# A two-layer streaming encoder on one core: part of the query/key group moved to the first pieces, the last piece reordered, one output chunk split in three passes

## The chip, the cores and the metric

The kernel runs on one core of one Trainium2 chip. The metric is the device time of one execution in microseconds. Five engines work beside each other, each on its own queue of instructions in a fixed order: TensorE (PE, with its weight loads as PEld), VectorE (DVE), ScalarE (ACT), GpSimd (POOL) and SyncE (SP), which here issues the large DMAs. A queue's instruction waits for semaphores of the others; what stands behind it waits too.

## The reference

One sequence of 256 tokens, 2048 channels, two layers, float32. All weights are read once, so the kernel streams them. Per layer, cut to what matters:

```python
mod = (c_act @ w_mod[l] + b_mod[l]).reshape(bn, 6, d)      # w_mod: 2048 x 12288
shift_m, scale_m, gate_m = mod[:, 0, None], mod[:, 1, None], mod[:, 2, None]
h = layer_norm(x) * (1.0 + scale_m) + shift_m
proj = h @ w_in[l]
uv, q_c, kv_c, k_r, sb, sc, sh, ag = jnp.split(proj, IN_SPLITS, axis=-1)
y_a = gmlp_mixer(uv, ...)            # gelu, layer norm of v, 128 x 128 mixing over tokens, u * mixed
y_b = mla_mixer(q_c, kv_c, k_r, ...) # latent attention
y_c = short_conv_mixer(sb, sc, sh, sconv_w[l])
y_d = conformer_conv(ag, ...)        # a * sigmoid(g), 31 taps over tokens, layer norm, silu
y = jnp.concatenate([y_a, y_b, y_c, y_d], axis=-1) @ w_out[l]
x = layer_norm(ALPHA * x + (1.0 + gate_m) * y, post_mix_g[l], post_mix_b[l])
...
y = conv_ffn(h, ffn_w_up[l], ffn_w_conv[l], ffn_b_conv[l], ffn_w_down[l])
x = layer_norm(ALPHA * x + (1.0 + gate_f) * y, post_ffn_g[l], post_ffn_b[l])
```

## The kernel before

**Products.** Weights stream in k tiles of 128 rows. A product is either exact (float32 operands, weights straight from DMA in tiles called `wexact`) or 3-pass: the weights arrive in a raw buffer (`wraw`, 4 buffers that the `wmod` transfers share), ScalarE casts them to fp32r (`whi`, L453), VectorE subtracts to get the rest (`wlo`, L454), the activations are split in the same way (`hT`), and three products hi x hi, hi x lo, lo x hi are summed in one PSUM bank. `mm` (L83) records every product.

**Modulation.** `w_mod` is summed over its rows on VectorE: a transfer `wmod`, then steps `qacc` or `macc` (L248) on it; a product with ones and small copies make `mod`, the scale and shift. Layer 0's normalised input needs scale and shift before any product, so it is done in pieces.

**Layer 0 in pieces** (`by_pieces`). `PIECES` cuts the 16 k tiles into (0, 2), (2, 2), (4, 4), (8, 4), (12, 4); a piece waits only for the modulation of its own channels (`between`). In each piece run four column groups: D (w_in's convolution columns, 1024 wide, summed over all pieces in the four PSUM banks `D0_c0` to `D0_c3`), U and V (512 wide each, the gMLP's halves) and E (512 wide, the short convolution's gate). D's products are cut in four parts, with U, V, E between them. The first `PLAIN_KT` = 4 k tiles, pieces 0 and 1, are exact for all groups; the rest of D is 3-pass, and U, V and E are 3-pass only in the last piece. U, V and E do not keep banks between the pieces: `side` computes a piece into two fresh banks, and their running sums lie in SBUF (`sumU`, `sumV`, `sumE`): in piece 0 ScalarE copies the banks there, in middle pieces it copies a bank to `part` (L1289) and VectorE adds (L1290), in the last VectorE adds from the bank (L1286).

**After the pieces** follow `mix_d` (sigmoid `sg` on ScalarE and product `gluD` on VectorE, L869 and L870, then 31 taps), `mix_u` (gelu `ya`, L954) and `mix_v` (gelu `va`, L977; transposed gMLP weights `ps_wT`, `wT`; layer norm; products `ps_mix`). A tap is four products `prodD` on ScalarE (L902) with one add into `convD` on VectorE; the first tap is an ACTIVATE into `convD` itself. There are two `prodD` buffers. The taps lie in the list `background`, from which the later groups pop a few per unit of weights (`STEPS`). Sigmoid and gelu each need their own table in ScalarE (ACT_TABLE_LOAD).

**Group B** (`group` with C_Q, 768 columns: query and key-value latents, exact, banks `B0_c0` to `B0_c2`, 8 units of 2 k tiles), then group C (1024 columns), then the output projection (`out_proj`) in column chunks 0 to 1024, 1024 to 1536 and 1536 to 2048; there `plain` tells how many units of a chunk are exact.

**The rest of w_mod** is spread over the units of these groups: `RATES[0]` tells how many transfers with their `macc` step are issued per unit (`pump`).

The order on each engine's queue is set by a scheduler from the program's order and the dependences.

```python
PIECES = ((0, 2), (2, 2), (4, 4), (8, 4), (12, 4))
CHUNKS = ((0, 1024), (1024, 512), (1536, 512))
rawp = ctx.enter_context(tc.tile_pool(name="rawp", bufs=4))
```

Of the kernel before, what the change touches and what calls it, by code (L numbers as in the profile page):

```python
# [54 lines left out]
def encoder_kernel(ctx: ExitStack, tc: tile.TileContext, A: dict, consts: bass.AP, out: bass.AP):  # L55
# [23 lines left out]
    def acc_tile(name):  # L79
        return accp.tile([P, 512], F32, tag="acc", name=name)  # L80
# [392 lines left out]
        act.copy(hi, src)  # L473
        dve.tensor_tensor(out=lo, in0=src, in1=hi.bitcast(F32), op=ALU.subtract)  # L474

    def group(w, c0, width, name, then, ntm=0, nk=2, hF=None, bg=0, spare=0):

        ncm = (width - 512 * ntm) // P  # L480
        box = {}

        def products(item, u):
            if u == 0:
                box["c"] = [acc_tile(f"{name}_c{i}") for i in range((ncm + 1) // 2)]
                box["t"] = [[acc_tile(f"{name}_t{t}{i}") for i in range(ntm)] for t in range(2)]
                box["h"] = list(hT)
            for part in (range(0, min(4, ncm)), range(4, ncm)):
                for k, (hi, lo) in enumerate(item):
                    kt = u * nk + k  # L490
                    st, sp = kt == 0, kt == KT - 1
                    for i in part:
                        o = box["c"][i // 2][:, (i % 2) * S : (i % 2 + 1) * S]
                        off = slice(i * P, (i + 1) * P)
                        first = st and i % 2 == 0
                        if lo is None:
                            mm(o, hi[:, off], hF(kt), first, sp)
                        else:
                            xh, xl = (h[:, kt % 2, :] for h in box["h"][kt // 2][:2])
                            mm(o, hi[:, off], xh, first, False)  # L500
                            mm(o, hi[:, off], xl, False, False)
                            mm(o, lo[:, off], xh, False, sp)
            for k, (hi, lo) in enumerate(item):
                kt = u * nk + k
                st, sp = kt == 0, kt == KT - 1
                for i in range(ntm):
                    off = slice(ncm * P + i * 512, ncm * P + (i + 1) * 512)
                    for t in range(2):
                        tok = slice(t * P, (t + 1) * P)
                        o = box["t"][t][i]  # L510
                        if lo is None:
                            mm(o, hF(kt)[:, tok], hi[:, off], st, sp)
                        else:
                            xh, xl = (h[:, kt % 2, tok] for h in box["h"][kt // 2][:2])
                            mm(o, xh, hi[:, off], st, False)
                            mm(o, xh, lo[:, off], False, False)
                            mm(o, xl, hi[:, off], False, sp)

        def load(u, spare=spare):
            return weights(w, u * nk, nk, c0, width, hF is not None, spare if u == 0 else 0)  # L520

        def end():
            then(box["c"], box["t"])

        return KT // nk, load, products, end, bg

    def group2(w, c0, name, then, bg=0, spare=0):

# [19 lines left out]
        def load(u):  # L548
            return weights(w, u * nk, nk, c0, 512, False, spare if u == 0 else 0)

        return KT // nk, load, products, lambda: then(box["c"]), bg

    def run(g):
        units, load, products, end, bg = g
        for u in range(units):
            stream(lambda: load(u), lambda item, u=u: products(item, u), bg)
        pending.append(end)

# [684 lines left out]
    def by_pieces(l, w_in, hF, between, mix_d, mix_u, mix_v, mix_b, mix_c, mix_e):  # L1243
# [12 lines left out]
        def terms(kt, part):  # L1256

            hi, lo = part
            if lo is None:
                return [(hi, hf(kt))]  # L1260
            xh, xl = (h[:, kt % 2, :] for h in hT[kt // 2][:2])
            return [(hi, xh), (hi, xl), (lo, xh)]
# [6 lines left out]
                    mm(o, w[:, i * P : (i + 1) * P], x, first and n == 0 and i % 2 == 0, last and n == len(ts) - 1)  # L1269

        def side(g, parts, k0, nkt):
            ps = [acc_tile(f"{g}{l}_{i}") for i in range(2)]
            for kt, part in parts:
                st, sp = kt == k0, kt == k0 + nkt - 1
                if g == "V":
                    ts = terms(kt, part)
                    for t in range(2):
                        for n, (w, x) in enumerate(ts):
                            mm(ps[t], x[:, t * P : (t + 1) * P], w, st and n == 0, sp and n == len(ts) - 1)
                else:  # L1280
                    chan_major(ps, kt, part, range(4), st, sp)
            for i in range(2):
                if k0 == 0:
                    act.copy(sums[g][i], ps[i])
                elif k0 + nkt == KT:
                    dve.tensor_tensor(out=sums[g][i], in0=ps[i], in1=sums[g][i], op=ALU.add)  # L1286
                else:
                    part = tmp_tile("part")
                    act.copy(part, ps[i])  # L1289
                    dve.tensor_tensor(out=sums[g][i], in0=part, in1=sums[g][i], op=ALU.add)  # L1290

        first = between(0)[1]
        first()
        for q, (k0, nkt) in enumerate(PIECES):
# [3 lines left out]

            def load(g, kt):

                c0, width = (C_AG, 1024) if g == "D" else (cols[g], 512)
                nk = min(2048 // width, nkt)
# [38 lines left out]
        def mix_ce(cps, tps):  # L1341
# [162 lines left out]
    for l in range(DEPTH):  # L1504
# [4 lines left out]
        else:  # L1509
# [97 lines left out]
```

## Time and profile before

| | |
|---|---|
| time, median of 3 runs | 2297.42 us (2294.97 to 2298.74) |
| the profiled execution's own time | 2298.88 us |
| its span | 2297.1 us |
| mean TensorE clock granted | 0.987 of full |
| TensorE busy | 97% of the span |
| the five pieces of layer 0 | until about 191 us |
| group B, then C, then output, layer 0 | from about 191, 235 and 327 us; output until about 432 us |
| the rest (feed-forward of layer 0, layer 1) | from about 432 us |

A profile row names the engine, the line, the operation and output<-inputs by the program's names. Times are from the span's start. An exact product shows as two matmul instructions, a 3-pass one as three. Idle time before a row stands in brackets with what ended it. The chain of waits is followed back from the last instruction and shows what the end hung on.

### The profile page before, as it was taken

What the parts mean: (1) busy time and instruction counts of PE and PEld (TensorE: products, weight loads), DVE (VectorE), ACT (ScalarE), POOL (GpSimd) and SP (SyncE); (2) the same over time, 40 slices, a digit from 0 to 9 for tenths busy, and PEclk for the clock granted to TensorE, in tenths of its full rate; (3) what the DMA queues carried; (4) which work ended last, traced back from release to release, by engine and by line L of the source; (5) the groups of instructions that cost most, each with busy time, mean ns of one, the idle gap of its engine ahead of it and who ended that gap; (6) DMA issues with size and microseconds to landing.
All of it is one profiled execution on the core that took longest, in us unless ns stands there. A gap on an engine that the chain in (4) does not pass through costs nothing.

```text
span 2297.1 us, 31478 instructions
## 1 busy us (share of the span) xinstructions
PE 2238.4 (97%) x12387; PEld 1934.1 (84%) x12387; DVE 1790.7 (78%) x2211; ACT 1071.6 (47%) x1597; POOL 34.4 (1%) x65
## 2 busy tenths in 40 slices
PE   6899999999999999999999999999999999999998
PEld 4688886798888888888789999889888888888886
DVE  6878987778888888998977899796676565565676
ACT  2235742335454544544455435545454454454553
POOL 2000000000000000000000000000000000000000
PEclk9899999999999999999999999999999999999999
DMA  9999788777889888898857677875665555555554
GB/s 344 362 340 343 271 321 333 263 278 279 317 303 335 292 326 318 303 354 307 311 186 260 202 238 252 291 260 185 249 243 202 193 178 197 192 193 185 188 195 147
DMA packets 228717, 605.21 MB, mean 263 GB/s; under 512 B 14660, under 2 KB 27188, under 8 KB 210900
## 3 DMA queue, kind: packets, MB, share of 16 engines
q1 hardware_dynamic: 227784, 602.30, 73.7%
q8 instruction: 97, 1.59, 0.3%
q0 software_dynamic: 784, 0.90, 0.1%
q14 instruction: 52, 0.43, 0.0%
HBM read 601.05 MB, written 2.10 MB: 263 GB/s over the span
## 4 chain that ended last, share of the span: by engine, by line
PE 89%; DVE 5%; DMA 3%; issue 1%; ACT 1%; SPq 0%; POOL 0%; DVEq 0%; POOLq 0%; ACTq 0%
PE g_c L83 21%; PE v_c L83 21%; PE d L83 20%; PE o L83 8%; PE D_c L83 4%; PE C_c L83 4%; PE B_c L83 3%; DMA wmod<-in_w_mod_dram 2%; PE U_c L83 1%; DVE wlo L454 1%; PE U L83 1%; PE E L83 1%; PE ps_mod L83 1%; PE E_c L83 1%; DVE qacc L248 1%
## 5 line engine op out<-in xcount | busy, mean ns | idle before, releaser
L453 ACT CAST whi<-wraw 128x1024 fp32r<-128x1024 f32 (+1 forms) x632 | 643.6, 1043 | 780.4 <-PE g_c L83 210.0
L454 DVE TENSOR_TENSOR wlo<-wraw,whi 128x1024 fp32r<-128x1024 f32 (+1 forms) x632 | 750.6, 1214 | 292.2 <-ACT whi L453 278.3
L83 PE MATMUL d<-whi,a 128*128 128x512 f32 x1344 | 390.6, 392 | 0.9 <-ACT whi L453 0.9
L248 DVE SCALAR_TENSOR_TENSOR macc<-wmod,cact,macc 128x2048 f32<-128x2048 f32 (+2 forms) x174 | 353.8, 2033 | 32.3 <-DMA wmod<-in_w_mod_dram 31.7
L83 PE MATMUL v_c<-hT,whi 128*128 128x512 f32 (+1 forms) x1456 | 343.1, 383 | 0.0
L83 PE MATMUL g_c<-hT,whi 128*128 128x512 f32 (+1 forms) x1344 | 313.3, 380 | 0.0
L83 PEld LDWEIGHTS v_c<-hT,whi 128*128 128x128 f32 x1456 | 264.6, 189 | 48.5
L83 PEld LDWEIGHTS d<-whi,a 128*128 128x128 f32 x1344 | 253.2, 189 | 54.6 <-ACT whi L453 2.2
L83 PEld LDWEIGHTS g_c<-hT,whi 128*128 128x128 f32 x1344 | 243.4, 189 | 43.2
L83 PE MATMUL d<-wlo,a 128*128 128x512 f32 x672 | 234.4, 392 | 1.6 <-DVE wlo L454 1.6
L83 PE MATMUL v_c<-hT,wlo 128*128 128x256 f32 x1400 | 190.7, 283 | 0.0
L83 PEld LDWEIGHTS v_c<-hT,wlo 128*128 128x128 f32 x1400 | 183.1, 191 | 6.6
L83 PE MATMUL g_c<-hT,wlo 128*128 128x256 f32 x1280 | 175.8, 283 | 0.0
L83 PEld LDWEIGHTS g_c<-hT,wlo 128*128 128x128 f32 x1280 | 168.2, 191 | 5.9
L83 PEld LDWEIGHTS d<-wlo,a 128*128 128x128 f32 x672 | 127.0, 189 | 30.3 <-DVE wlo L454 3.9
L473 ACT CAST a<-g 128x512 fp32r<-128x512 f32 x132 | 80.8, 619 | 91.0 <-PE d L83 89.3
L83 PE MATMUL o<-whi,a 128*128 128x512 f32 x384 | 112.4, 398 | 0.8 <-ACT whi L453 0.8
L474 DVE TENSOR_TENSOR a<-g,a 128x512 fp32r<-128x512 f32 x132 | 87.7, 685 | 9.5 <-ACT a L473 9.5
L83 PEld LDWEIGHTS o<-whi,a 128*128 128x128 f32 x384 | 73.1, 191 | 17.5 <-ACT whi L453 1.2
L83 PE MATMUL D_c<-hT,whi 128*128 128x256 f32 x432 | 82.0, 290 | 2.8 <-ACT hT L473 2.3
L248 DVE SCALAR_TENSOR_TENSOR qacc<-wmod,cact,qacc 128x1024 f32<-128x1024 f32 (+1 forms) x75 | 80.3, 1070 | 2.6 <-DMA wmod<-in_w_mod_dram 0.5
L1364 DVE SCALAR_TENSOR_TENSOR u<-g,pf,u 128x254 f32<-128x254 f32 (+1 forms) x176 | 73.5, 476 | 3.0 <-ACT u L86 3.0
(371 smaller groups left out, 2603.7 us busy)
## 6 DMA issues: line engine op xcount, KB each, us to landing
wraw<-in_ffn_w_up_dram SPq DMA_DIRECT2D x168, 1024.0 KB, 5.0
wmod<-in_w_mod_dram SPq DMA_DIRECT2D x134, 1024.0 KB, 6.2
wraw<-in_ffn_w_down_dram SPq DMA_DIRECT2D x88, 1024.0 KB, 5.2
wraw<-in_w_in_dram SPq DMA_DIRECT2D x33, 1024.0 KB, 6.9
wmod<-in_w_mod_dram SPq DMA_DIRECT2D x64, 512.0 KB, 9.2
wraw<-in_w_out_dram SPq DMA_DIRECT2D x26, 1024.0 KB, 6.7
wmod<-in_w_mod_dram SPq DMA_DIRECT2D x32, 768.0 KB, 6.6
wexact<-in_w_in_dram SPq DMA_DIRECT2D x46, 512.0 KB, 7.4
```

The source lines that it names most:

```text
L83: pe.matmul(o, lhsT, rhs, start=start, stop=stop, skip_group_check=True)
L248: i = dve.scalar_tensor_tensor(out=acc, in0=w, scalar=col, in1=acc, op0=ALU.mult, op1=ALU.add)
L453: act.copy(hi[:, :m], r)
L454: i = dve.tensor_tensor(out=lo[:, :m], in0=r, in1=hi[:, :m].bitcast(F32), op=ALU.subtract)
L473: act.copy(hi, src)
L474: dve.tensor_tensor(out=lo, in0=src, in1=hi.bitcast(F32), op=ALU.subtract)
L1364: dve.scalar_tensor_tensor(out=u[:, sh:], in0=x[:, : S - sh], scalar=col(k, j), in1=u[:, sh:], op0=ALU.mult, op1=ALU.add)
```

## The change

1. `RATES[0]`: w_mod transfers per unit B 1.6 to 1.634, C 1.9 to 2.2, output 1.7 to 1.5.
2. Group B's first 4 k tiles are computed in pieces 0 and 1, as a side group "B" after V (sums in two new slots, `sumB0` and `sumB1`). Group B then begins at unit 2 of 8, and ScalarE copies those sums into its banks first (L490).
3. `side` handles its banks one after the other. From piece 1 on ScalarE copies the running sum into the bank (L1280), the products are summed onto it, and ScalarE copies the bank back (L1292). VectorE's adds are gone. U's final banks are not copied back: `mix_u` reads them.
4. In the last piece D is computed in full first and `mix_d` is called at once; then for U, V and E: the load, one w_mod transfer, two of `background`'s taps, and the products.
5. Output, second chunk: its first two units (8 k tiles, the y of groups A and B) are 3-pass instead of exact.

```diff
-    dict(B=1.6, C=1.9, out=1.7, first=1.2, up=0.68, down=0.83),
+    dict(B=1.634, C=2.2, out=1.5, first=1.2, up=0.68, down=0.83),
...
-    def group(w, c0, width, name, then, ntm=0, nk=2, hF=None, bg=0, spare=0):
+    def group(w, c0, width, name, then, ntm=0, nk=2, hF=None, bg=0, spare=0, begun=None):
...
+        skip = 0 if begun is None else PLAIN_KT // nk
+
         def products(item, u):
-            if u == 0:
+            if u == skip:
                 box["c"] = [acc_tile(f"{name}_c{i}") for i in range((ncm + 1) // 2)]
+                if begun is not None:
+                    for bank, part in zip(box["c"], begun):
+                        act.copy(bank, part)
...
-        return KT // nk, load, products, end, bg
+        return range(skip, KT // nk), load, products, end, bg
...
-        cols = {"U": C_UV, "V": C_UV + 512, "E": C_SB}
+        cols = {"U": (C_UV, 512), "V": (C_UV + 512, 512), "E": (C_SB, 512), "B": (C_Q, 768)}
...
         def side(g, parts, k0, nkt):
-            ps = [acc_tile(f"{g}{l}_{i}") for i in range(2)]
-            for kt, part in parts:
-                st, sp = kt == k0, kt == k0 + nkt - 1
-                if g == "V":
-                    ts = terms(kt, part)
-                    for t in range(2):
+            for i, total in enumerate(sums[g]):
+                o = acc_tile(f"{g}{l}_{i}")
+                if k0 > 0:
+                    act.copy(o, total)
+                for kt, part in parts:
+                    st, sp = kt == 0, kt == k0 + nkt - 1
+                    if g == "V":
+                        ts = terms(kt, part)
                         for n, (w, x) in enumerate(ts):
-                            mm(ps[t], x[:, t * P : (t + 1) * P], w, st and n == 0, sp and n == len(ts) - 1)
+                            mm(o, x[:, i * P : (i + 1) * P], w, st and n == 0, sp and n == len(ts) - 1)
+                    else:
+                        chan_major([None] * i + [o], kt, part, (2 * i, 2 * i + 1), st, sp)
+                if g == "U" and k0 + nkt == KT:
+                    u_banks.append(o)
                 else:
-                    chan_major(ps, kt, part, range(4), st, sp)
-            for i in range(2):
-                if k0 == 0:
-                    act.copy(sums[g][i], ps[i])
-                elif k0 + nkt == KT:
-                    dve.tensor_tensor(out=sums[g][i], in0=ps[i], in1=sums[g][i], op=ALU.add)
-                else:
-                    part = tmp_tile("part")
-                    act.copy(part, ps[i])
-                    dve.tensor_tensor(out=sums[g][i], in0=part, in1=sums[g][i], op=ALU.add)
+                    act.copy(total, o)
+            if u_banks and g == "U":
+                mix_u(u_banks, None)
...
+            if k0 + nkt == KT:
+                for kt, half in turns_d:
+                    d_part(kt, half)
+                mix_d(accD, None)
+                for g in "UVE":
+                    load(g, k0)
+                    next(mods)
+                    for _ in range(2):
+                        background.pop(0)()
+                    side(g, [(kt, loaded[(g, kt)]) for kt in range(k0, KT)], k0, nkt)
+                continue
             for s in range(4):
...
-                if s < 3:
-                    g = "UVE"[s]
+                for g in ("U", "VB" if exact else "V", "E", "")[s]:
                     load(g, k0)
-                    some_mods((0.5, 0.85, 1.0)[s])
+                    some_mods((0.5, 0.85, 1.0, 1.0)[s])
                     side(g, [(kt, loaded[(g, kt)]) for kt in range(k0, k0 + nkt)], k0, nkt)
-        mix_d(accD, None)
-        mix_u(sums["U"], None)
         mix_v(None, [[x] for x in sums["V"]])
         phase(l, "B")
-        run(group(w_in, C_Q, 768, f"B{l}", mix_b, hF=hf, bg=STEPS[l]["B"]))
+        run(group(w_in, C_Q, 768, f"B{l}", mix_b, hF=hf, bg=STEPS[l]["B"], begun=sums["B"]))
...
-            plain={1024: 2, 1536: 4} if l == 0 else {},
+            plain={1536: 4} if l == 0 else {},
```

How the instructions stand now. On TensorE in piece 1, from V to E, before (names are output<-weights or activations, then the size; x counts equal ones):

```order
L83 MATMUL V0_0_461<-wexact_454,hF0_115 128x512
L83 MATMUL V0_1_462<-wexact_454,hF0_115 128x512
L83 MATMUL V0_0_461<-wexact_454,hF0_115 128x512
L83 MATMUL V0_1_462<-wexact_454,hF0_115 128x512
L83 MATMUL E0_0_484<-hF0_115,wexact_482 128x256 x2
L83 MATMUL E0_1_485<-hF0_115,wexact_482 128x256 x2
```

and now:

```order
L83 MATMUL V0_0_483<-wexact_476,hF0_115 128x512 x2
L83 MATMUL V0_1_488<-wexact_476,hF0_115 128x512 x2
L83 MATMUL B0_0_497<-hF0_115,wexact_493 128x256 x2
L83 MATMUL B0_0_497<-hF0_115,wexact_495 128x256 x2
L83 MATMUL B0_1_504<-hF0_115,wexact_493 128x256 x2
L83 MATMUL B0_1_504<-hF0_115,wexact_495 128x256 x2
L83 MATMUL B0_2_511<-hF0_115,wexact_493 128x256 x2
L83 MATMUL B0_2_511<-hF0_115,wexact_495 128x256 x2
L83 MATMUL E0_0_529<-hF0_115,wexact_527 128x256 x4
L83 MATMUL E0_1_536<-hF0_115,wexact_527 128x256 x4
```

Twelve products of B have come between V and E, and each bank is finished before the next begins.

On ScalarE at the end of the last piece, before:

```order
L453 CAST whi_1240<-wraw_1234 128x1024
L869 ACT_TABLE_LOAD
L869 ACTIVATE sg_1321<-D0_c2_121 128x512
L869 ACTIVATE sg_1324<-D0_c3_122 128x512
L954 ACT_TABLE_LOAD
L954 ACTIVATE ya_1328<-sumU_129 128x512 x2
L977 ACTIVATE va_1337<-sumV_130 128x512 x2
L86 ACTIVATE convD_1327<-gluD_1320,pm0_111 128x256 x4
L902 ACTIVATE prodD_1396<-gluD_1320,pm0_111 128x255 x4
```

and now, from the sigmoid to the copy of V's sum into its first bank, `V0_0`, on which V's products of this piece are summed:

```order
L874 ACTIVATE sg_1193<-D0_c3_122 128x512
L453 CAST whi_1282<-wraw_1276 128x1024
L86 ACTIVATE convD_1196<-gluD_1189,pm0_111 128x256 x4
L907 ACTIVATE prodD_1215<-gluD_1189,pm0_111 128x255 x4
L959 ACT_TABLE_LOAD
L959 ACTIVATE ya_1273<-U0_0_1221 128x512
L959 ACTIVATE ya_1273<-U0_1_1247 128x512
L907 ACTIVATE prodD_1289<-gluD_1189,pm0_111 128x253
L907 ACTIVATE prodD_1215<-gluD_1189,pm0_111 128x254 x4
L907 ACTIVATE prodD_1289<-gluD_1189,pm0_111 128x253 x3
L1280 COPY V0_0_1300<-sumV_130 128x512
L1280 COPY V0_1_1315<-sumV_130 128x512
```

The sigmoid, the taps' first products and the gelu of U have moved ahead of the copies that V waits for.

On VectorE at the same place, before:

```order
L248 SCALAR_TENSOR_TENSOR macc_1388<-wmod_1454,cact_104,macc_1388 128x2048
L1286 TENSOR_TENSOR sumE_131<-E0_0_1244,sumE_131 128x512
L1286 TENSOR_TENSOR sumE_131<-E0_1_1245,sumE_131 128x512
L870 TENSOR_TENSOR gluD_1320<-D0_c0_119,sg_1321 128x512
L870 TENSOR_TENSOR gluD_1320<-D0_c1_120,sg_1324 128x512
L248 SCALAR_TENSOR_TENSOR macc_1388<-wmod_1483,cact_104,macc_1388 128x2048
L982 COPY wT_1340<-ps_wT_1341 128x512
```

and now:

```order
L454 TENSOR_TENSOR wlo_1279<-wraw_1276,whi_1278 128x1024
L248 SCALAR_TENSOR_TENSOR macc_1207<-wmod_1286,cact_104,macc_1207 128x2048
L875 TENSOR_TENSOR gluD_1189<-D0_c0_119,sg_1190 128x512
L875 TENSOR_TENSOR gluD_1189<-D0_c1_120,sg_1193 128x512
L454 TENSOR_TENSOR wlo_1283<-wraw_1276,whi_1282 128x1024
L248 SCALAR_TENSOR_TENSOR macc_1207<-wmod_1340,cact_104,macc_1207 128x2048
L908 TENSOR_TENSOR convD_1196<-convD_1196,prodD_1215 128x4x255
L248 SCALAR_TENSOR_TENSOR macc_1207<-wmod_1464,cact_104,macc_1207 128x2048
L908 TENSOR_TENSOR convD_1196<-convD_1196,prodD_1215 128x4x254
L248 SCALAR_TENSOR_TENSOR macc_1207<-wmod_1499,cact_104,macc_1207 128x2048
```

Modulation steps now stand ahead of `gluD` and between the tap adds, whose completion frees a `prodD` buffer.

More of the change, by code (lines that the diff above doesn't have):

```diff
@@ L549, in load @@
             return weights(w, u * nk, nk, c0, 512, False, spare if u == 0 else 0)
-        return KT // nk, load, products, lambda: then(box["c"]), bg
+        return range(KT // nk), load, products, lambda: then(box["c"]), bg
     def run(g):
         units, load, products, end, bg = g
-        for u in range(units):
+        for u in units:
             stream(lambda: load(u), lambda item, u=u: products(item, u), bg)
@@ L1271, in side @@
         def side(g, parts, k0, nkt):
[L1272 to L1290 removed]
+            for i, total in enumerate(sums[g]):
[6 more added lines that the diff above has]
+                        ts = terms(kt, part)
+                        for n, (w, x) in enumerate(ts):
+                            mm(o, x[:, i * P : (i + 1) * P], w, st and n == 0, sp and n == len(ts) - 1)
[3 more added lines that the diff above has]
+                    u_banks.append(o)
+                else:
+                    act.copy(total, o)
+            if u_banks and g == "U":
+                mix_u(u_banks, None)
+        u_banks = []
+        both = [slot("sumB0"), slot("sumB1")]
+        sums["B"] = [both[i // 2][:, (i % 2) * 512 : (i % 2 + 1) * 512] for i in range(3)]
         first = between(0)[1]
@@ L1299, in load @@
             def load(g, kt):
-                c0, width = (C_AG, 1024) if g == "D" else (cols[g], 512)
-                nk = min(2048 // width, nkt)
+                c0, width = (C_AG, 1024) if g == "D" else cols[g]
+                nk = min(max(2, 2048 // width), nkt) if exact else min(2048 // width, nkt)
                 for j, p in enumerate(weights(w_in, kt, nk, c0, width, exact or (g != "D" and q < len(PIECES) - 1))):
```

## The prediction

> **What bounds the kernel now.** I read the page's first part, then busy time by stage, then TensorE's own rows where a stage is not full. First the page:
>
> ```profile
> PE 2238.4 (97%) x12387; PEld 1934.1 (84%) x12387; DVE 1790.7 (78%) x2211; ACT 1071.6 (47%) x1597; POOL 34.4 (1%) x65
> ```
>
> TensorE is busy 97% of the span, so a change pays by taking instructions off it or by filling its gaps. In the stretches that the edits touch (columns: stretch and length, then busy us of PE, weight load, DVE, ACT, POOL, then TensorE clock, DMA share, GB/s):
>
> ```profile
> 62.00:85.00 23.00, 16.36 (x61) 11.16 (x59) 19.58 (x22) 7.18 (x14) 0.00 (x0) 0.85 1.01 370
> 85.00:122.00 37.00, 34.44 (x168) 28.30 (x168) 29.32 (x28) 7.93 (x12) 0.00 (x0) 0.91 1.00 371
> 122.00:162.00 40.00, 38.29 (x222) 31.87 (x221) 32.48 (x34) 12.48 (x22) 0.00 (x0) 1.00 0.98 353
> 191.00:235.00 44.00, 43.67 (x212) 38.36 (x210) 41.45 (x40) 29.69 (x69) 2.56 (x5) 1.00 1.01 368
> 375.00:399.00 24.00, 24.00 (x73) 13.57 (x72) 22.65 (x23) 3.99 (x4) 0.00 (x0) 1.00 1.00 375
> ```
>
> The pieces (62 to 162) are the loose part: 10.9 us without a matmul (23.00 - 16.36, 37.00 - 34.44, 40.00 - 38.29), and a clock of 0.85 and 0.91 in two of the stretches, while DMA is full. Group B (191 to 235) is full on TensorE, VectorE and DMA at once. The output's second chunk (375 to 399) is full on TensorE, and VectorE is nearly so. TensorE's rows (start, length, what, and in brackets its idle time and what ended it):
>
> ```profile
> 61.70 3.62 PE L83 MATMUL U<-hF,wexact 128*128 128x256 f32 x16
> 67.75 5.37 PE L83 MATMUL V<-wexact,hF 128*128 128x512 f32 x8 [2.43 <-DMA wexact<-in_w_in_dram]
> 75.15 5.38 PE L83 MATMUL E<-hF,wexact 128*128 128x256 f32 x16 [2.04 <-DMA wexact<-in_w_in_dram]
> ...
> 109.96 0.58 PE L83 MATMUL D_c<-hT,wlo 128*128 128x256 f32 x1 [2.56 <-DVE wlo L454]
> ...
> 191.17 8.80 PE L83 MATMUL B_c<-hF,wexact 128*128 128x256 f32 x40
> 200.30 0.71 PE L83 MATMUL ps_mix<-wT,va 128*128 128x128 f32 x4 [0.33 <-DVE va L991]
> ...
> 363.95 2.07 PE L83 MATMUL o<-whi,a 128*128 128x512 f32 x4 [0.76 <-ACT whi L453]
> ```
>
> And the chain of waits, which gives steady pitches and one DMA that the chain waits for as group B begins:
>
> ```profile
> 185.94 7.75 DMA wmod<-in_w_mod_dram
> ...
> 202.79 32.38 PE B_c L83 x150
> ...
> 327.03 32.70 PE o L83 x144
> ...
> 411.58 20.72 PE o L83 x48
> ```
>
> Pitches: an exact product, 256 wide, is two instructions of 32.38/150 = 0.216 us; an exact one, 512 wide, two of 20.72/48 = 0.432; a 3-pass one, 512 wide, three of 32.70/144 = 0.227.
>
> **The change part by part.**
>
> *Group B's first 4 k tiles move into pieces 0 and 1.* Six blocks by 4 k tiles are 24 exact products, 48 instructions: 48 x 0.216 = 10.4 us leave group B, where TensorE has no gap. The bank copies that now open the group are counted with the last piece. The same 48 are issued earlier, 5.2 us in each piece. There they delay TensorE by 10.4 us against four things that can go. The waits of 2.43 and 2.04 for weights: the weights come meanwhile. The slow stretches after them: eight instructions of V at 0.432 are 3.5 against 5.37, 16 of E at U's rate 3.62 against 5.38, so 1.9 + 1.8. The later wait of 2.56 for a split half, and smaller ones. That is 10.7 us, so TensorE comes out even, if the data come. Against it stands DMA: 4 x 128 x 768 x 4 bytes = 1.57 MB more before 122 us, at 370 GB/s 4.2 us, in queues that are full.
>
> *The adds of the sums go.* What made VectorE late with the split halves was this:
>
> ```profile
> L1290 DVE TENSOR_TENSOR sumU<-part,sumU x6: 684/692/694, 65.1 to 138.3; 128x512 f32<-128x512 f32 x6
> L1290 DVE TENSOR_TENSOR sumV<-part,sumV x6: 682/684/685, 75.3 to 149.6; 128x512 f32<-128x512 f32 x6
> L1290 DVE TENSOR_TENSOR sumE<-part,sumE x6: 686/691/692, 80.3 to 158.3; 128x512 f32<-128x512 f32 x6
> ```
>
> ```profile
> 99.42 0.69 DVE L1290 TENSOR_TENSOR sumU<-part,sumU 128x512 f32<-128x512 f32 x1 [3.24 <-ACT part L1289]
> 100.28 0.69 DVE L1290 TENSOR_TENSOR sumU<-part,sumU 128x512 f32<-128x512 f32 x1 [0.17 <-ACT part L1289]
> 100.89 7.88 DVE L248 SCALAR_TENSOR_TENSOR qacc<-wmod,cact,qacc 128x1024 f32<-128x1024 f32 x6
> 108.69 1.22 DVE L454 TENSOR_TENSOR wlo<-wraw,whi 128x1024 fp32r<-128x1024 f32 x1
> ```
>
> 18 adds are 12.4 us, and the add stands on VectorE waiting 3.24 for TensorE's bank with six modulation steps (7.88) and then a split half behind it, for which TensorE waits at 109.96. ScalarE copies the bank instead, both ways, and VectorE no longer waits for TensorE there; raw buffers come free earlier, which gives DMA back part of its 4.2. Bounds: all 4.2 us late (a loss) or 3.5 us early (the 2.56 and small waits, uncovered). I take 1.0 us of gain on top of the 10.4, since the row at 109.96 sits in the piece that decides.
>
> *The last piece.* Now D is done first and its mixing starts behind it, with U, V, E after. The taps then run beside products, and the price is a queue. Rows of ScalarE and VectorE for the same operations:
>
> ```profile
> 190.21 1.32 ACT L869 ACTIVATE sg<-D_c 128x512 f32<-128x512 f32 x2 [8.67 <-PE D_c L83]
> 191.55 1.28 ACT L954 ACT_TABLE_LOAD   x1
> 192.84 1.15 ACT L954 ACTIVATE ya<-sumU 128x512 f32<-128x512 f32 x2
> 193.90 1.13 ACT L977 ACTIVATE va<-sumV 128x512 f32<-128x512 f32 x2
> 194.94 2.06 ACT L86 ACTIVATE convD<-gluD,pm 128x256 f32<-128x256 f32 x4
> 196.91 3.27 ACT L902 ACTIVATE prodD<-gluD,pm 128x255 f32<-128x255 f32 x8
> ```
>
> ```profile
> 190.84 1.41 DVE L870 TENSOR_TENSOR gluD<-D_c,sg 128x512 f32<-128x512 f32 x2 [1.62 <-ACT sg L869]
> 193.79 2.35 DVE L248 SCALAR_TENSOR_TENSOR macc<-wmod,cact,macc 128x2048 f32<-128x2048 f32 x1 [1.53 <-DMA wmod<-in_w_mod_dram]
> ```
>
> ```profile
> L1289 ACT COPY part<-U x6: 586/586/587, 64.5 to 137.7; 128x512 f32<-128x512 f32 x6
> ```
>
> V's first bank cannot start before ScalarE has copied the old sum into it, and on ScalarE that copy stands behind the whole first part of the mixing. Count from D's end. Before, gluD ended at 192.25, 1.5 us after TensorE's last D; now a modulation step (2.35) stands ahead of it on VectorE, so 1.5 to 3.9: I take 2.7. Then on ScalarE: convD 2.06, four tap products 4 x 0.41, table load 1.28, ya 1.15, eight tap products 8 x 0.41, one bank copy 0.59: 10.0. V can start at 12.7. TensorE has only U's two banks to do, 48 instructions of 0.12 (a 3-pass product 256 wide is half of one 512 wide, 3 x 0.227/2 = 0.34), 5.8 us: it waits 6.9. From V's copy to the first copy of group B, ScalarE has another 13.9 us (two casts 2.1, 16 tap products 6.6, seven bank copies 4.1, va 1.1) against 11.3 us of V and E: 2.6 more. The gMLP product waited 0.33 before; with va now split by the queue I give 1.3. The slow stretch after the long gap is priced by the rows at 67.75 and 75.15, 1.8 to 1.9 after gaps half as long: 1.9. Loss: 6.9 + 2.6 + 1.0 + 1.9 = 12.4 us. Bounds: 4, if the first wait and its slow stretch do not come (2.6 + 1.0 stay), to 20, if a modulation step that stands between the tap adds waits for its DMA as at 193.79 or longer (7.75 from issue to landing, in the chain).
>
> The Trainium skill ("TensorE: Matmul & The Clock Gate", Part 1: The HAM clock gate) says that half clock comes after one idle window of about 3.4 us and lasts about 3.4 us of work. This trace shows slow products behind gaps of only 2.43 and 2.04 us, so the window here is not a floor; by the page the penalty would be about 1.7 (an estimate, half of 3.4) where the rows give 1.9, and the sum would move by 0.2.
>
> The skill's "ScalarE: Activation LUTs" (What ACT_TABLE_LOAD costs) adds about 1.38 us of draining to each load of 1.28. Here the ACTIVATE at 192.84 follows the load of 191.55 by 1.29, with no drain between. By the page the wait for V would be 8.3, and the sum 1.4 us worse.
>
> *Mixing rates.* In the output's first chunk fewer w_mod steps (1.5 for 1.7 a unit) stand among the casts that TensorE waited 0.76 for at 363.95, and the four instructions there took 2.07 where 4 x 0.227 is 0.9. Both may go: 1.5, from 0 to 3. Group C gets more steps (2.2 for 1.9); VectorE's spare time hides them: 0, with 1.5 to both sides.
>
> *The output's second chunk.* 16 products go from two instructions of 0.432 to three of 0.227: 16 x (0.864 - 0.681) = 2.9 us less TensorE work. It adds four casts on ScalarE (idle: 3.99 busy of 24) and four subtractions of 1.22 on VectorE, 4.9 us, where it is 22.65 of 24 busy. TensorE may wait for the first pair: I keep half, 1.5, from -1 to 2.9.
>
> Sum: -10.4 - 1.0 + 12.4 - 1.5 + 0 - 1.5 = -2.0 us. The profiled execution took 2298.88 us (span 2297.1) and would be 2296.9; the median of the runs shown is 2297.42, 1.46 below it, which gives 2295.4.
>
> **The rivals.** Under 0.2% (4.6 us) a difference cannot be told from none here.
>
> *The wait in the last piece is small.* If V's copy comes while U runs (the loss at its lower bound, 4), the sum is -10.4, and the median 2287. For it: ScalarE is only 29.69 of 44 busy in the stretch behind. Against it: the queue's order and the rows' durations add up to 12.7 against 5.8 with no slack assumed.
>
> *It grows (slower).* A modulation step stands on VectorE between two tap adds; ScalarE's next products need the buffer that the add frees; V, E and group B's copies stand behind. With DMA full, one w_mod transfer late by its 7.75 us makes the loss 20.2: -2.0 + 7.8 = +5.8, median 2303. It decides once the lateness passes 6.6 us. For it: the chain ran through such a transfer before. Against it: four raw buffers let transfers run ahead of the steps that use them, and weights drop out of group B.
>
> *DMA bounds the pieces.* The 1.57 MB arrive 4.2 us late in full and the adds' removal gives nothing back: 5.2 us worse, +3.2, median 2301, unmeasurable. For it: shares of 1.00 and 1.01. Against it: VectorE's stalls, not DMA, held the raw buffers.
>
> *The 3-pass chunk turns into VectorE's wait:* at its bound it takes 2.5 us of the forecast, same class.
>
> **How the numbers follow.** The sum as it stands, with DMA and chunk variations of a few us: 0.43, centred on 2295.4, own range 2291 to 2300. The wait small: 0.29. The wait grown: 0.16. DMA bound: 0.12. The small-wait case reaches faster by over 0.2% nearly always (0.27), the sum as it stands in a quarter (0.10): 0.37. Slower: 0.14 from the grown wait, 0.04 from DMA bound with anything else wrong, 0.01 besides: 0.19. The rest, 0.44, is within 0.2%. The range leaves out a fifth, the tails of the two outer cases: 2286 to 2303.
>
> **What would show it.** TensorE should issue B products between V and E in the first two pieces, V and E there without their waits of 2.43 and 2.04; group B should take 144 instructions, about 31 us. In the last piece a wait of V for ScalarE's copy, near 7 us, with a lower clock behind, shows the main loss right; none shows it wrong. Group B should end near 235 as before. In the second output chunk ya and yb should show three instructions of 0.227 and a wait for a split half under 1.5. The prediction is wrong most easily in the length of ScalarE's queue, or in DMA's time for the earlier weights.

## The result, and the profile after

The changed kernel takes 2291.76 us (median of 7 runs, 2288.11 to 2293.81) against 2297.42 before: a ratio of 0.9973, with a 95% interval of 0.9963 to 0.9983. It is 5.7 us faster. The profiled execution has a span of 2290.0 us. Single executions of one kernel differ by some 5 us, so many of the comparisons below are read from places in the profile rather than from the total. A place in one profile has a spread too: nine profiles of kernels that are alike up to the end of the pieces put it between 155.56 and 157.53 us.

The same stretches as before (stretch and length, then busy us of PE, weight load, DVE, ACT, POOL, then clock, DMA share, GB/s):

```profile
62.00:85.00 23.00, 22.99 (x108) 18.30 (x106) 18.31 (x15) 11.49 (x21) 1.90 (x4) 1.00 1.04 386
85.00:122.00 37.00, 34.30 (x166) 28.16 (x166) 26.13 (x25) 13.32 (x22) 0.00 (x0) 0.91 1.05 390
122.00:162.00 40.00, 39.70 (x237) 33.73 (x238) 29.17 (x30) 17.36 (x32) 0.00 (x0) 1.00 1.02 382
162.00:191.00 29.00, 23.19 (x153) 21.34 (x153) 25.59 (x20) 22.84 (x40) 0.00 (x0) 0.82 0.79 290
191.00:235.00 44.00, 44.00 (x245) 39.73 (x244) 40.29 (x43) 31.42 (x79) 2.84 (x5) 1.00 0.96 352
...
375.00:399.00 24.00, 23.70 (x99) 18.54 (x100) 23.93 (x23) 6.01 (x6) 0.00 (x0) 1.00 0.93 320
```

In the first stretch TensorE's gaps are gone (22.99 of 23 where 16.36 was busy). In the second they are not: it is busy for 34.30 of 37 at a clock of 0.91, much as before (34.44 and 0.91). DMA moves 386 and 390 GB/s where it moved 370 and 371. The last piece (162 to 191) is now the loose part: 23.19 of 29 busy, at a clock of 0.82. Before it was full:

```profile
162.00:191.00 29.00, 28.87 (x219) 27.91 (x220) 21.76 (x20) 9.79 (x12) 0.00 (x0) 1.00 0.78 276
```

On TensorE now:

```profile
70.49 3.67 PE L83 MATMUL V<-wexact,hF 128*128 128x512 f32 x8
74.17 5.47 PE L83 MATMUL B<-hF,wexact 128*128 128x256 f32 x24
79.48 3.62 PE L83 MATMUL E<-hF,wexact 128*128 128x256 f32 x16
...
183.26 0.45 PE L986 MATMUL ps_wT<-cst,gmlp 128*128 128x128 f32 x1 [5.06 <-DMA gmlp<-in_gmlp_w_s_dram]
```

V and E in piece 1 lost their waits of 2.43 and 2.04 and run at full pace; 24 instructions of B stand between. In the last piece TensorE waits 5.06 us, and the row blames the transfer of the gMLP weights. The chain of waits, which follows what each step was released by, tells it differently:

```profile
171.70 1.44 DVE macc L248
173.14 0.82 issue
173.96 0.69 DVE gluD L875
174.66 0.02 issue
174.68 2.08 ACT convD L86 x4
176.76 1.59 ACT prodD L907 x4
178.36 0.02 issue
178.37 1.28 ACT L959
179.66 0.01 issue
179.67 1.08 ACT ya L959 x2
180.75 3.16 ACT prodD L907 x8
183.91 0.49 ACT V L1280
184.40 0.04 issue
184.45 8.50 PE V L83 x24
192.95 5.76 PE E L83 x48
```

That is the predicted queue, step by step: w_mod step, `gluD`, first tap, tap products, table load, gelu, eight tap products, the copy into V's bank. Two waits end within 1.2 us of each other (183.26 and 184.45), and the profile can name only the one that came last for each instruction. The next section takes them apart.

Where the time went, by places in TensorE's rows (us from the span's start). The first of them, the start of the last scale and shift products, is called the pieces' end below:

| | before | changed |
|---|---|---|
| last scale and shift products of the pieces begin | 157.50 | 156.21 |
| group B's first product | 191.17 | 198.87 |
| group B's last product ends | 235.16 | 231.96 |
| group C's last product ends | 327.03 | 323.29 |
| feed-forward part's first product | 434.33 | 429.15 |

### The profile page after: what moved, and what is told of

It reads as the page before. It is cut to its first block, busy times and chain, and to the rows that moved or that the text cites. A ratio compares the mean times of both kernels' runs of the same rounds, so it can differ in the third digit from the quotient of the medians.

```text
span 2290.0 us, 31538 instructions
## 1 busy us (share of the span) xinstructions
PE 2235.1 (98%) x12403; PEld 1935.5 (85%) x12403; DVE 1780.2 (78%) x2191; ACT 1097.2 (48%) x1641; POOL 34.4 (2%) x65
## 4 chain that ended last, share of the span: by engine, by line
PE 86%; DVE 7%; DMA 4%; ACT 2%; issue 1%; POOL 0%; SPq 0%; DVEq 0%; ACTq 0%; POOLq 0%
PE g_c L83 22%; PE v_c L83 21%; PE d L83 20%; PE o L83 4%; PE D_c L83 4%; PE C_c L83 3%; DMA wmod<-in_w_mod_dram 2%; DVE wlo L454 2%; PE B_c L83 1%; PE U_c L83 1%; PE E L83 1%; DVE convD L886 1%; PE V L83 1%; PE ps_mod L83 1%; DVE macc L248 1%
## 5 line engine op out<-in xcount | busy, mean ns | idle before, releaser
L83 PE MATMUL o<-whi,a 128*128 128x512 f32 x416 | 120.7, 394 | 0.7 <-ACT whi L453 0.7
L83 PEld LDWEIGHTS o<-whi,a 128*128 128x128 f32 x416 | 78.6, 189 | 18.2 <-ACT whi L453 1.3
L83 PEld LDWEIGHTS D_c<-hT,whi 128*128 128x128 f32 x432 | 69.7, 197 | 4.7 <-ACT hT L473 1.7
```

The lines of the kernel that those rows point to most:

```text
L83: pe.matmul(o, lhsT, rhs, start=start, stop=stop, skip_group_check=True)
```

## The experiments

**Which wait holds V in the last piece?** First the gMLP weights early:

```diff
...
             if k0 + nkt == KT:
+                load_gmlp()
                 for kt, half in turns_d:
```

> The gMLP weights are loaded ahead of the last piece's D products instead of behind its w_mod transfers; nothing else. Theory A (ScalarE's queue holds V: the copy of V's sum stands behind the first taps): V still begins about 6.2 us after U's last product, now waiting for the copy alone, and the time stays at the changed kernel's 2291.8, within 1 us. Theory B (the transfer that the profile names, 5.06 us, holds V): the gap falls below 1.2 us, and the time by about 5 us, more if the slow stretch behind it goes, to 2284 to 2287.

Measured: 2291.59 us, ratio to before 0.9978 (0.9969 to 0.9987). TensorE's waits (waiting, what for, total us, times, longest):

```profile
PE V L83 <- ACT V L1286: 5.0, 1, 5.0
```

V begins at 185.00, 5.5 us behind U's last product where it was 6.25, and its whole wait now has ScalarE's copy as its cause. The transfer was a second wait under the same cover, and the time did not fall: theory A. Then the copy early:

```diff
...
                     next(mods)
+                    ps = banks_of(g) if g == "V" else None
                     for _ in range(2):
                         background.pop(0)()
-                    side(g, [(kt, loaded[(g, kt)]) for kt in range(k0, KT)], k0, nkt)
+                    side(g, [(kt, loaded[(g, kt)]) for kt in range(k0, KT)], k0, nkt, ps)
```

> The copies of V's sum into its two banks are issued ahead of the two taps that V's turn takes from the list, so on ScalarE they follow the gelu of U at once; the transposes of the gMLP weights come behind V on TensorE. Theory A: V begins right behind the gelu and one copy, at about 181.3 instead of 184.45, a gap of 3.1 us; the time falls by 3 to 5 us, to 2287 to 2289. Theory B: with the transposes out of the way V begins with U's end, and the time falls by 6 to 9 us. If the clock's drop comes from any gap of 2 us or more, the slow stretch behind V's start remains.

Measured: 2293.43 us, ratio 0.9985 (0.9975 to 0.9996), no gain on the changed kernel.

```profile
PE E L83 <- ACT E L1286: 4.0, 1, 4.0
PE V L83 <- ACT V L1279: 3.1, 1, 3.1
```

V began at 181.44, where 181.3 was expected, after a gap of 3.1. But the time did not fall: E now waits 4.0 for the copy into its own bank, and group B begins at 199.95, later than in the changed kernel. The expectation stopped at V; the same queue stands in front of E. With everything made ready for V (the gMLP weights early too):

```diff
...
+                load_gmlp()
+                pre = {"U": banks_of("U")}
+                load("U", k0)
+                load("V", k0)
                 mix_d(accD, None)
+                pre["V"] = banks_of("V")
                 for g in "UVE":
-                    load(g, k0)
+                    if g == "V":
+                        load("E", k0)
                     next(mods)
+                    ps = pre.get(g)
...
```

> All of it: gMLP weights early, U's and V's weights loaded ahead of the mixing, V's bank copies right behind the sigmoid, E's weights ahead of V's products. Theory A: V begins at U's end, no gap of 6.2, no slow stretch of 3.0: 9 us faster than the changed kernel, 2283, if nothing gives it back. Rival C: groups B and C then wait for taps on VectorE, and only part stays: 2286 to 2289. Theory B differs not here.

Measured: 2289.63 us, ratio 0.9968 (0.9956 to 0.9979). In the total that is no gain clear of the intervals. V begins at U's end with no gap, and E waits 3.34 us. The chain there:

```profile
185.96 0.79 ACT prodD L907 x2
186.75 0.95 ACT sumV L1304 x2
187.70 0.49 ACT E L1292
188.19 0.04 issue
188.23 8.59 PE E L83 x48
```

E's wait and its slow products (8.59 us where 5.76 stood in the changed kernel) take back 6.2 of the 9 us, and at group B's first product 2.2 are left (196.66 against 198.87; this profile's pieces end 0.8 later). What sets this piece is ScalarE's queue through to E's copy, not the place of V's copy in it. Neither theory had that.

**What is the last piece's order worth?**

```diff
-            if k0 + nkt == KT:
-                for kt, half in turns_d:
-                    d_part(kt, half)
-                mix_d(accD, None)
-                ...
-                continue
...
+        mix_d(accD, None)
         mix_v(None, [[x] for x in sums["V"]])
```

> The changed kernel with the last piece as before (D in four parts with U, V, E between, its mixing at the end; B=2.134 in the rates so that w_mod keeps its place). The gap in front of V and its slow stretch go: the last piece takes 29 us instead of 38.5. Theory A alone: 9.4 us faster, 2282. Rival C (VectorE becomes the bound): the eight taps that now run in the last piece fall into group B, which got 11 us shorter; VectorE has some 130 us of work in groups B and C against 125 of TensorE, so at least 5 us come back as waits before the convolution's norm: 2287 to 2292.

The rate of group B is 2.134 here (and in the later runs with the old last piece and a shortened group B), so that the w_mod transfers keep their places.

Measured: 2289.66 us, ratio 0.9965 (0.9952 to 0.9977). Group B begins at 189.49 (9.4 earlier than in the changed kernel) and ends at 223.34 (8.6 earlier), group C ends at 319.55 (3.7 earlier). So the old order loses 4.9 us again by the end of group C. There, TensorE waits for VectorE's rotary products, which stand behind a w_mod step and a late tap:

```profile
240.76 2.34 DVE L248 SCALAR_TENSOR_TENSOR macc<-wmod,cact,macc 128x2048 f32<-128x2048 f32 x1
243.03 1.15 DVE L908 TENSOR_TENSOR convD<-convD,prodD 128x956 f32<-128x956 f32 x1
244.09 0.42 DVE L1104 TENSOR_TENSOR qc<-ps_qr,cst 128x256 f32<-128x256 f32 x1
244.43 0.41 DVE L1105 TENSOR_TENSOR qc<-ps_qr,cst 128x256 f32<-128x256 f32 x1
...
244.98 0.67 PE L83 MATMUL ps_qr<-qc,cst 128*128 128x256 f32 x2 [2.28 <-DVE qc L1105]
```

This is rival C: taps that the new order puts beside U, V and E otherwise make VectorE late in group C. TensorE's waits from group B's end to group C's come to 3.3 us, and its clock there is 0.98 where the changed kernel has 1.00. The run with bank copies alone, below, has the old last piece too, but group B in full length, and shows no such wait: it comes with the shortened group B. The new order costs 8.6 us at one place and earns 4.9 at the next; the time lies where that rival put it. In the total the difference is not clear of the intervals.

**The two edits in the pieces, one without the other.** B's products moved, the adds kept (against the kernel before, cut):

```diff
...
+            for i, total in enumerate(sums[g]):
+                o = acc_tile(f"{g}{l}_{i}")
+                ... # products into the fresh bank o
+                if k0 == 0:
+                    act.copy(total, o)
+                elif k0 + nkt == KT:
+                    dve.tensor_tensor(out=total, in0=o, in1=total, op=ALU.add)
+                else:
+                    part = tmp_tile("part")
+                    act.copy(part, o)
+                    dve.tensor_tensor(out=total, in0=part, in1=total, op=ALU.add)
```

> The kernel before with group B's first 4 k tiles in pieces 0 and 1 alone: side groups one bank after the other, but with VectorE's adds of the sums as before, the last piece, the rates (B=2.134 for 6 units, so that w_mod keeps its place) and the output's second chunk as before. Theory A (the adds' stalls on VectorE hold back the split halves and the raw buffers, so the bank copies are what makes room for the moved products): the last piece begins 3 to 5 us later than before's 162, group B is 10.4 shorter, 5 to 7 us net at its end. Rival (DMA and VectorE have the room anyway, the gaps of 2.43, 2.04 and 2.56 take the products): the last piece begins at 161 to 163 and 9 to 10 us net reach the end of group B. Behind it the taps are late on VectorE, and the time falls by 3 to 6 us against before.

Measured: 2300.62 us, ratio 1.0015 (1.0006 to 1.0024): slower. And the bank copies on the kernel before (cut):

```diff
...
+            for i, total in enumerate(sums[g]):
+                o = acc_tile(f"{g}{l}_{i}")
+                if k0 > 0:
+                    act.copy(o, total)
+                ... # products onto it
+                    act.copy(total, o)
```

> The kernel before with the bank copies alone (ScalarE copies the running sum into the bank and back; no adds on VectorE; one bank after the other). Theory A: TensorE's wait of 2.56 for a split half and the smaller ones go, the last piece begins 2 to 4 us earlier than 162, and the time falls by 1 to 4 us. Rival (DMA, at a share of 1.00, bounds the pieces): the last piece begins within 1 us of before, and the time stays within 1.5 us.

Measured: 2288.43 us, ratio 0.9966 (0.9955 to 0.9977): bank copies alone give as much as the whole change, as far as the intervals tell. The pieces' end shows both edits: before, B moved with adds, and bank copies alone, in this order:

```profile
157.50 1.84 PE L83 MATMUL ps_mod<-onesR,qacc 128*128 128x1 f32 x16
```

```profile
168.08 1.84 PE L83 MATMUL ps_mod<-onesR,qacc 128*128 128x1 f32 x16
```

```profile
150.97 1.84 PE L83 MATMUL ps_mod<-onesR,qacc 128*128 128x1 f32 x16
```

The moved products cost 10.6 us in the pieces while the adds stand there, which is all that group B saves: it ends at 235.03 against 235.16. (Both runs also work through their banks one after the other, which the kernel before does not; what that alone does is not shown.) The rest of its loss comes later: group C ends 2.2 us behind the kernel before, and the feed-forward part begins 4.9 behind. Theory A had the direction, but expected 5 to 7 us to be left; nothing was. With the bank copies the products cost 5.2 (156.21 in the changed kernel, 150.97 without them). And the copies by themselves end the pieces 6.5 us earlier, where theory A gave them 2 to 4, and group B 7.2 (227.97). How they do it: between 60 and 160 us, first before and then with bank copies, the longest waits of SP's queue for a raw buffer of the w_mod transfers:

```profile
SPq L263 <- DVE qacc L248: 41.1, 15, 6.9
```

```profile
SPq L263 <- DVE qacc L248: 27.2, 15, 2.8
```

and VectorE's waits for copied banks, with B moved and the adds kept:

```profile
DVE sumU L1294 <- ACT part L1293: 11.7, 5, 4.6
DVE sumE L1294 <- ACT part L1293: 4.2, 1, 4.2
```

In the kernel before these two are 7.5 and 3.2. With bank copies no such row is left on VectorE. Its waits as such do not go: those for casts grow from 4.8 us to 16.8. What changes is what stands behind a wait. With bank copies the modulation steps in piece 1 run in one row, and VectorE waits when they are done:

```profile
59.12 15.81 DVE L248 SCALAR_TENSOR_TENSOR qacc<-wmod,cact,qacc 128x1024 f32<-128x1024 f32 x12
79.02 1.23 DVE L454 TENSOR_TENSOR wlo<-wraw,whi 128x1024 fp32r<-128x1024 f32 x1 [4.08 <-ACT whi L453]
```

Before, four adds stand among these steps, the first after a wait of 1.53 us for its bank, and the last step ends at 79.0 instead of 74.9. In the next piece, with the wait of 3.24 that the prediction shows, the last step ends at 114.8 instead of 109.3. So an add that waited for TensorE's bank held up the modulation steps behind it, and these held the raw buffers. DMA moved less for it although its share read 1.01: with bank copies it moved 388 GB/s instead of 370 in the same stretch, 62 to 85 us, in which TensorE was no busier:

```profile
62.00:85.00 23.00, 15.93 (x66) 11.70 (x66) 17.76 (x18) 11.22 (x20) 0.00 (x0) 0.91 1.04 388
```

**Chunk and rates.** The output's second chunk exact again:

```diff
-            plain={1536: 4} if l == 0 else {},
+            plain={1024: 2, 1536: 4} if l == 0 else {},
```

> The changed kernel with the output's second chunk exact in its first two units again. If half of the 2.9 us of TensorE work was lost to a wait for split halves, as predicted, the output takes 1.5 us longer than in the changed kernel's profile (104.2 from its first to its last product); if all of the saving was real, 2.9; if VectorE gave it all back, 0.

Measured: 2292.74 us, ratio 0.9985 (0.9975 to 0.9995); the changed kernel's interval, 0.9963 to 0.9983, overlaps. From the output's first to its last product this profile shows 102.3 us against 104.2, shorter and not longer. The chunk's gain is not clear of zero. In the changed kernel TensorE waits 0.75 us for a split half there, and this profile has no such wait. The old rates:

```diff
-    dict(B=1.634, C=2.2, out=1.5, first=1.2, up=0.68, down=0.83),
+    dict(B=1.6, C=1.9, out=1.7, first=1.2, up=0.68, down=0.83),
```

> The changed kernel with the old rates (B=1.6, C=1.9, output 1.7 w_mod transfers per unit). As predicted, group C stays the same and the output's first chunk takes 1.5 us longer, by the wait of 0.76 for a cast and the slow products behind it; if the rates cost nothing in the output, within 0.5 us. The time then goes up by 0 to 2 us.

Measured: 2301.78 us, ratio 1.0023 (1.0014 to 1.0032): 10 us slower than the changed kernel, far outside what was expected. Yet at the feed-forward's first product it stands at 430.05 against 429.15. The loss is behind all that the change touches. The rates' sum, 6 x 1.6 + 8 x 1.9 + 12 x 1.7 + 3 = 48.2, differs from 48.404 by a fifth of a transfer, and with it where w_mod steps fall among the later units. With the sum kept (B=1.634, the rest old):

> The changed kernel with the old rates in groups C and output (C=1.9, output 1.7) and B=1.634 kept, so that the sum of transfers is again 48.404. The run with B=1.6 took 10 us more than the changed kernel, of which only 1 was there at the feed-forward's first product. If that came from the sum alone (48.2, a fifth of a transfer, which shifts where w_mod steps fall among the feed-forward's units), this kernel is 2 to 4 us slower than the changed one, by the output: 2294 to 2296. Rival (the rates of C and output themselves cost 10): 2301.

Measured: 2295.71 us, ratio 0.9992 (0.9982 to 1.0002), as expected. So 6 of the 10 us came from the sum, and 4 from the rates of C and output, though the interval just touches the changed kernel's. From the output's first product to the feed-forward's first it takes 111.0 us against 106.2. What the shift by a fifth of a transfer moves is not shown: the largest difference between these two profiles stands in layer 0's up projection (520.4 us from its first product to the first down product with the shift, 516.7 without), but seven profiles of other kernels without it show 515.5 to 519.2 there. The same new rates on the kernel with bank copies alone:

```diff
-    dict(B=1.6, C=1.9, out=1.7, first=1.2, up=0.68, down=0.83),
+    dict(B=1.6, C=2.2, out=1.5, first=1.2, up=0.68, down=0.83),
```

> The kernel before with the bank copies and with the new rates in groups C and output (C=2.2, output 1.5; B stays 1.6 for its 8 units, so that the sum of w_mod transfers up to the feed-forward part, 48.4, is unchanged). Bank copies alone gave 2288.4, with the last group of the output part ending about 105 to 109 us after its first product. If the rates are what shortens the output by 3 to 4 us (the profiles with the new rates show 102.6 to 106.2 from the output's first product to the feed-forward's first, those with the old ones 107.6 to 110.3), the time falls to 2284 to 2286. Rival (that difference is from profile to profile, not from the rates): 2288.

Measured: 2291.48 us, ratio 0.9979 (0.9970 to 0.9989): no gain on 0.9966; the rival held. The rates earn 4 us in the changed kernel and nothing here in the total, where the second chunk is exact. The output itself is shorter with them all the same. From its first product to the feed-forward's first, the eight profiles with the new rates show 102.6 to 107.8 us (mean 105.3) and the five with the old ones 107.7 to 111.0 (mean 109.2); these kernels differ in other things too. TensorE's waits between 318 and 440 us with the old rates and the 3-pass chunk (the run before this one):

```profile
PE ps_xT L592 <- ACT xn L86: 2.5, 1, 2.5
PE o L83 <- ACT whi L453: 1.0, 1, 1.0
PE o L83 <- DVE wlo L454: 0.8, 1, 0.8
```

The changed kernel has no wait for a cast (`whi`) there, much the same for a split half (1.0 in two), and waits of 0.8 at most for `xn`, the normed rows behind the output. The other run with the old rates and the 3-pass chunk has the same three waits (2.5, 0.8, 0.8). So the split half is not what the rates ease; what makes `xn` late with the old ones stays open. Last, bank copies, moved products and rates, without the last piece's order and the 3-pass chunk:

```diff
-            plain={1536: 4} if l == 0 else {},
+            plain={1024: 2, 1536: 4} if l == 0 else {},
```

(on top of the old last piece, and with B=2.134 again)

> The changed kernel without its last-piece order and with the output's second chunk exact: bank copies, moved B products and rates are left. Against the run with bank copies and rates it shows what the moved products are worth: at group B's end 4 to 5 us, in the whole 2 to 4, since the taps then make VectorE late in group C as in the run with the old last piece. Theory: 2283 to 2287. Rival (group C gives back all): no faster than bank copies and rates.

Measured: 2292.04 us, ratio 0.9976 (0.9965 to 0.9986). Group B ends at 222.08, 5.8 us ahead of the run with bank copies and rates (227.86), but group C ends at 320.24 against 319.30: it gave back all. The rival was right, and the expected 2283 to 2287 was missed.

## Why the prediction was right or wrong

The forecast was 2295.4 and, as the likeliest outcome, a change inside 0.2%; the time is 2291.76, inside the range and 0.27% faster, with an interval (0.17 to 0.37%) that still touches 0.2%. That the total came so near is partly luck: in the pieces two wrong terms cancelled. The largest difference that is left, 3.0 us of 3.6, is the last piece.

- **Group B shorter by 10.4: right.** From its first to its last product it takes 33.1 us instead of 44.0.
- **The moved products fit into the pieces for nothing: wrong as a term, and the size of the adds' removal with it.** The prediction let 10.7 us of waits and slow stretches pay for 10.4 us of products and gave the adds' removal 1.0. The runs show the products costing 5.2 (10.6 with the adds) and the removal giving 6.5. The two together made 1.3 at the pieces' end against 1.0 predicted, the right sum from wrong parts: luck. The mechanism of the removal was named rightly (adds at VectorE's head hold modulation steps and raw buffers). The step that failed was its price. It counted only what TensorE then waited for behind VectorE, at most 3.5 us; the 2.56 in it was used a second time to pay for the moved products, and the raw buffers were to give back only part of the 4.2 us of extra transfers. SP's queue waiting 41.1 us for raw buffers stood in the same profile; the prediction makes no term of it.
- **The last piece: mechanism right, one term too many.** V's wait was forecast at 6.9 us from a start at 12.7 behind D's end, with a lower clock behind it; U ended at 178.20 and V began at 184.45, 6.25 apart and 12.2 behind D's end (172.28), and the clock of the stretch is 0.82. The slow stretch was put at 1.9; V took 8.50 us, and in the kernel before

```profile
173.92 5.47 PE V L83 x24
```

  so it was 3.0. The 2.6 in front of group B did not come. ScalarE took 14.1 us from V's first copy (183.81) to group B's first (197.93), where 13.9 was forecast, but V and E took 14.3 and not 11.3: the slow stretch and ScalarE's lateness run beside each other, and the prediction added them. Nor did the 1.0 at the gMLP product come. Group B began 9.4 us later than with the old order, where 12.4 was forecast: that is the 3.0. Group B's end, forecast near 235, came at 231.96. The prediction also had no term for what the early taps earn in group C, 4.9 us against the run with the old last piece; the changed kernel's C took 91.3 us, the kernel before's 91.9.
- **Rates 1.5, chunk 1.5.** By places the two together gave 1.5 in the output, half of what was forecast (group C's end is 3.7 earlier, the feed-forward's first product 5.2). Taken apart, the rates are worth about 4, in the total of this kernel and as the difference of the two means above, where 1.5 was forecast and 3 was the bound; the wait for a cast that they were to remove is gone. The chunk is worth nothing that is clear of the intervals; its wait of 0.75 for a split half is inside what was forecast. One profile of each kernel does not settle how they share the output's 1.5.
- **Clock and table load.** A gap of 3.10 us was followed by V at full pace (181.44 to 187.02 for 24 instructions) in the run with V's copy early, and a gap of 3.06 by slow products in the run with bank copies alone, where 16 instructions of E took 5.38 us instead of 3.62. Gaps of 3.34 and more had slow products behind them, and so had gaps of 2.43 and 2.04 in the kernel before. By "TensorE: Matmul & The Clock Gate" (the Trainium skill, Part 1: The HAM clock gate) slow products follow an idle window of about 3.4 us, and the window runs on its own clock. The traces agree that the length of a gap alone does not decide; but a gap of 2.04 or 2.43 cannot fill such a window, so by these traces the window need not be idle throughout, and what it counts no run here shows. In the changed kernel the table load at 178.37 follows the last tap product by 0.02 us, and the gelu starts 1.30 behind the load's start. The drain that "ScalarE: Activation LUTs" (the Trainium skill, What ACT_TABLE_LOAD costs) adds to a table load is again not there.

## What to carry to other kernels

An instruction that waits at the head of an in-order queue costs what stands behind it: take the running sum into the PSUM bank on an engine with time, and the engine that feeds the transfers keeps feeding them. A full DMA share did not mean here that DMA was the limit; look at what SP's queue waits for. When a wait in front of one product is removed, follow the same queue to the next product before counting the gain. And before two delays on different engines are added, ask whether they run beside each other.

## What the runs showed of the hardware that was not expected

Two gaps of TensorE of the same length had different clocks behind them: after 3.10 us V ran at full pace (24 instructions in 5.6 us), after 3.06 us E did not:

```profile
73.49 5.38 PE L83 MATMUL E<-hF,wexact 128*128 128x256 f32 x16 [3.06 <-DMA wexact<-in_w_in_dram]
```

A shift by a fifth of one transfer in the w_mod stream was worth 6 us in the total (2301.78 against 2295.71); why is not shown. And DMA at a share of 1.01 still had room: 370 GB/s before, 388 with its buffers freed earlier.
